# Start of a decoder layer: scale before shift, and the adaLN product's k tiles on four column strips

## The chip, the cores and the metric

The kernel runs on one core of one Trainium2 chip. The metric is device time in microseconds (us), the median of several runs. Five engines work side by side, each through its own instructions in order: TensorE (PE, with PEld for its weight loads), VectorE (DVE), ScalarE (ACT), GpSimd (POOL) and SyncE (SP), which here issues loads and stores.

## The reference

One decoder layer for 512 prompt rows and 8 sequences of 4 sample rows, 544 rows in all, of 1024 features each. Only its first steps are touched:

```python
def decoder_layer(x, c, pos, conv_buf, S0, attend, p):
    mod = jax.nn.silu(c) @ p['w_ada'] + p['b_ada']
    sh1, sc1, g1, sh2, sc2, g2, sh3, sc3, g3 = [m[:, None, :] for m in jnp.split(mod, 3 * N_SUB, axis=-1)]
    h = rmsnorm(x, p['ffn1_norm_pre']) * (1 + sc1) + sh1
    x = x + 0.5 * g1 * rmsnorm(swiglu(h, p['ffn1_w_gate'], p['ffn1_w_up'], p['ffn1_w_down']), p['ffn1_norm_post'])
...
```

The vector c has 9 rows (one for the prompt, eight for the samples), and w_ada is 1024 x 9216: nine segments of 1024 columns, of which segment 0 is sh1 and segment 1 is sc1. Everything is float32.

## The kernel before

x is held transposed, features on partitions: `xT` is 128 partitions x 8 blocks x 544 columns (a column is a row of x). Columns come in two halves of 272; the last 32 of the second half are the sample rows, whose modulation differs per sequence. A float32 matmul is done as three matmuls in a one-pass format (L301, `mm3`): weights and activations are each split into a high part and a rest (`hi`, `lo` of the weights, L270 on ACT and L271 on DVE; `hh`, `hl` of the activations).

The start of the layer, up to the steady feed-forward, is what the change touches. Its steps:

- Loads. SP issues c, the five pieces of x, then tiles `wb` of w_ada (128 x 512, 256 KB), then the first feed-forward weight tiles `raw`. ACT's queue issues nine small loads of gains, biases and convolution weights (`vraw`, `wraw`). Loads take one of eight completion semaphores each; a load that takes a semaphore again waits until the load that had it last has landed.
- x is turned by PE (`xps`, L507), copied to `xT`, and its squares are summed (`sqx`, L525). The sum over features is a matmul (`pre_s`, L366); DVE works out the reciprocal root in a chain of small operations (L340 to L345); PE spreads it over partitions (`pre_p`, L353 and L355, one tile for each column half).
- adaLN. `ada` multiplies the transposed silu(c) (`cT`, 32 columns of stationary weights per k tile) by w_ada. It is called with two pieces, (segment 1, half h) and (segment 0, half h): for each k tile one matmul for each piece, on two of TensorE's four 32-column strips (`adaps`, L467). After 8 k tiles the result goes through ACT (`ms`, L471) and is turned by PE (`adapt`, L474); DVE adds the bias and forms the scale (`modT`, L480 and L488). A float32 matmul shows as two records in the profile.
- Modulate (L536 to L551). For each block of 128 features and each column half: DVE multiplies x by scale and root (`mt`, L536), ACT adds the shift and rounds (`hh`, L538), DVE forms the rest (`hl`, L539). The 32 sample columns of each block take four small DVE steps and one on ACT (`ts`, L545 to L551).
- The feed-forward starts with block 0 of 11: four units of 24 matmuls each (`pg` and `pu` over features 0 to 511, then over 512 to 1023). It is issued behind the modulation but mixed into it by the compiler's order, and a coroutine `rest` adds the other seven segments of w_ada (`wa` tiles, four pieces a time) between the feed-forward's matmuls.

A half h of the feature blocks (0 to 3, then 4 to 7) goes through adaLN and modulate in turn.

Of the kernel before, what the change touches and what calls it, by code (L numbers as in the profile page):

```python
# [19 lines left out]
P = 128  # L20
# [7 lines left out]
ST = 4  # L28
# [208 lines left out]
class Layer:  # L237
# [170 lines left out]
    def load_vectors(self, sp):  # L408
        nc, a = self.nc, self.a
        v = sp.tile([112, P], F32, name="vraw")  # L410
        nc.scalar.dma_start(out=v[0:72, :], in_=a["b_ada"][0].rearrange("(b c) -> b c", c=P))
        gains = ("ffn1_norm_pre", "ffn1_norm_post", "mix_norm_pre", "mix_norm_post", "ffn2_norm_pre")
        for i, n in enumerate(gains):
            nc.scalar.dma_start(out=v[72 + 8 * i:80 + 8 * i, :], in_=a[n][0].rearrange("(b c) -> b c", c=P))
        w = sp.tile([105, P], F32, name="wraw")
        nc.scalar.dma_start(out=w[0:96, :], in_=a["conv_w"][0].rearrange("i (b c) -> (i b) c", c=P))
        nc.scalar.dma_start(out=w[96:97, :], in_=a["dn_norm"])
        nc.scalar.dma_start(out=w[97:105, :], in_=a["ffn2_norm_post"][0].rearrange("(b c) -> b c", c=P))
        return v, w

    def use_vectors(self, v, w):
# [26 lines left out]
    def ada(self, pieces, wa_pool, whole=True):  # L448
# [28 lines left out]
        for j, (seg, h) in enumerate(pieces):  # L477
            bs = slice(4 * h, 4 * h + 4)
            m = self.modT[:, seg, bs, :]
            nc.vector.tensor_tensor(  # L480
                out=m, in0=ptv[:, :, 32 * j:32 * j + 9],
                in1=self.vecs[:, seg * 8 + 4 * h:seg * 8 + 4 * h + 4].unsqueeze(2).to_broadcast([P, 4, 9]), op=ALU.add)
            kind, sub = seg % 3, seg // 3
            if kind:
                gv = self.gains[("ffn1_norm_", "mix_norm_", "ffn2_norm_")[sub] + ("pre" if kind == 1 else "post")]
                gb = gv[:, bs].unsqueeze(2).to_broadcast([P, 4, 9])
                if kind == 1:
                    nc.vector.scalar_tensor_tensor(out=m, in0=m, scalar=1.0, in1=gb, op0=ALU.add, op1=ALU.mult)  # L488
                else:
                    nc.vector.scalar_tensor_tensor(out=m, in0=m, scalar=1.0 if sub == 1 else 0.5, in1=gb,  # L490
                                                   op0=ALU.mult, op1=ALU.mult)

    def smod(self, seg, b0, b1):

# [1304 lines left out]
def layer(ctx, tc, a, dbg=None, stop=None):  # L1799
# [25 lines left out]
    mx.plan(feed)  # L1825
    with ExitStack() as c2:
        sp = L.pool("sp", 1, c2)
        vw = L.load_vectors(sp)
        L.load_cond(sp)
        L.load_x(sp)  # L1830
        wa = L.pool("wa2", 24, c2)
        ada0 = L.ada([(1, 0), (0, 0)], wa, False)
        for b in range(8):
            for c in range(2):
                L.sumsq(L.xT[:, b, :], sqx, b, tmp, c, nc.vector if b % 2 else None)
            if b % 2:
                next(ada0)
        rms0 = L.rms(sqx, (0, 1), "pre0")
        for i in range(4):
            next(ada0)  # L1840
            if i == 1:
                with tc.issue_after(L.ada_mm.ins):
                    next(rms0)
                    L.use_vectors(*vw)
        with tc.issue_after(L.ada_mm.ins):
            rps = drain(rms0)
        drain(ada0)
        for i in range(4):
# [134 lines left out]
```

## Time and profile before

| | us |
|---|---|
| median of 3 runs | 1587.06 |
| lowest and highest | 1586.16, 1587.81 |
| the profiled execution | 1590.33 |
| its span, first to last instruction | 1588.5 |

The profile is of one execution. Its span is the time from the first to the last instruction that it shows; 1.8 us of that run lie outside it. TensorE is busy for 95% of the span and its granted clock is 0.981 on the mean, so a microsecond saved where TensorE waits, early in the program, shortens the whole run by a microsecond if nothing later takes it back. The change touches only the first 60 us of code; from about 140 us on the instructions of each engine stand in the same order as before.

### The profile page before, as it was taken

Reading aid. Unit: us, or ns where it says so; the run is one execution under the profiler, and the core shown is the slowest. Engines: PE = TensorE matmul, PEld = TensorE weight load, DVE = VectorE, ACT = ScalarE, POOL = GpSimd, SP = SyncE. Lnnn points to the kernel's source line nnn. Section 1 sums busy time; section 2 is a strip of 40 time slices with the busy share of each in tenths; the row PEclk is TensorE's granted clock in tenths of the full one; section 3 lists DMA queues with packets and bytes.
Section 4 is the critical chain, followed back from the end, with each engine's and each line's share of the span. In section 5 each row is a group of like instructions: output and inputs, shape, how many; then the busy total and the mean of one; then the engine's idle time right before and its main releaser. Section 6 shows DMA issues by size and latency. Waiting matters only on the chain. (4 is left out here: it accounts for less than half of the span.)

```text
span 1588.5 us, 32490 instructions
## 1 busy us (share of the span) xinstructions
PE 1513.1 (95%) x12819; PEld 1408.5 (89%) x12819; DVE 846.5 (53%) x2080; ACT 633.5 (40%) x1397; POOL 293.7 (18%) x386
## 2 busy tenths in 40 slices
PE   7999999999998999998999999998989999999996
PEld 3898999999987999898788898896979999999995
DVE  5433322333488787468879658748374332233354
ACT  4222222222445554254675432233465332233363
POOL 1000000000353232123012112312548000000042
PEclk9999999999999999799999999999999999999998
DMA  9455454554656434554212325624426323333253
GB/s 323 140 172 179 129 160 141 160 158 136 197 162 194 115 89 105 127 146 112 48 44 67 99 69 133 160 78 131 139 67 167 107 82 92 91 91 87 83 148 102
DMA packets 314533, 199.64 MB, mean 126 GB/s; under 512 B 36464, under 2 KB 297331, under 8 KB 314092
## 3 DMA queue, kind: packets, MB, share of 16 engines
q1 hardware_dynamic: 314086, 197.46, 43.7%
q8 instruction: 100, 1.64, 0.4%
q14 instruction: 53, 0.43, 0.1%
q10 hardware_dynamic: 294, 0.11, 0.0%
HBM read 182.08 MB, written 16.36 MB: 125 GB/s over the span
## 5 line engine op out<-in xcount | busy, mean ns | idle before, releaser
L270 ACT CAST hi<-raw 128x512 fp32r<-128x512 f32 (+2 forms) x502 | 287.0, 581 | 592.7 <-PE pu L301 161.8
L271 DVE TENSOR_TENSOR lo<-raw,hi 128x512 fp32r<-128x512 f32 (+2 forms) x368 | 249.9, 681 | 436.0 <-ACT hi L270 416.9
L301 PE MATMUL pb<-hh,hi 128*128 128x272 f32 (+1 forms) x1008 | 234.6, 303 | 2.2 <-ACT hh L270 1.8
L301 PE MATMUL pb<-hh,lo 128*128 128x272 f32 (+1 forms) x1008 | 226.5, 295 | 2.3 <-DVE lo L271 2.3
L301 PE MATMUL pb<-hl,hi 128*128 128x272 f32 (+1 forms) x1008 | 225.3, 294 | 0.0
L271 POOL TENSOR_TENSOR lo<-raw,hi 128x512 fp32r<-128x512 f32 (+1 forms) x104 | 139.1, 1341 | 450.9 <-ACT hi L270 423.6
L301 PEld LDWEIGHTS pb<-hh,hi 128*128 128x128 f32 (+1 forms) x1008 | 165.4, 192 | 12.1 <-issue 4.5
L301 PE MATMUL pd<-fh,hi 128*128 128x272 f32 x704 | 171.8, 291 | 0.0
L301 PE MATMUL pd<-fl,hi 128*128 128x272 f32 x704 | 170.9, 290 | 0.0
L301 PEld LDWEIGHTS pb<-hh,lo 128*128 128x128 f32 (+1 forms) x1008 | 165.0, 192 | 5.3 <-DVE lo L271 2.5
L301 PEld LDWEIGHTS pb<-hl,hi 128*128 128x128 f32 (+1 forms) x1008 | 165.2, 191 | 2.6 <-issue 1.0
L301 PE MATMUL pd<-fh,lo 128*128 128x272 f32 x672 | 162.2, 289 | 0.8 <-POOL lo L271 0.8
L301 PE MATMUL pg<-hh,hi 128*128 128x272 f32 x672 | 149.7, 293 | 7.1 <-ACT hh L550 3.4
L301 PE MATMUL pu<-hh,hi 128*128 128x272 f32 x672 | 148.8, 292 | 1.6 <-ACT hi L270 1.6
L301 PE MATMUL pg<-hl,hi 128*128 128x272 f32 x672 | 147.8, 290 | 0.8 <-DVE hl L539 0.7
L301 PE MATMUL pu<-hl,hi 128*128 128x272 f32 x672 | 146.5, 289 | 0.0
L301 PE MATMUL pu<-hh,lo 128*128 128x272 f32 x672 | 146.0, 289 | 0.0
L301 PE MATMUL pg<-hh,lo 128*128 128x272 f32 x672 | 145.8, 289 | 0.0
L301 PEld LDWEIGHTS pd<-fh,hi 128*128 128x128 f32 x704 | 120.6, 189 | 8.4 <-issue 5.9
L301 PEld LDWEIGHTS pg<-hh,hi 128*128 128x128 f32 x672 | 108.8, 189 | 19.4 <-ACT hh L550 5.4
L301 PEld LDWEIGHTS pd<-fl,hi 128*128 128x128 f32 x704 | 120.9, 189 | 0.0
L301 PEld LDWEIGHTS pu<-hh,hi 128*128 128x128 f32 x672 | 108.7, 190 | 11.2 <-issue 5.9
(445 smaller groups left out, 2508.5 us busy)
## 6 DMA issues: line engine op xcount, KB each, us to landing
raw<-w_in SPq DMA_DIRECT2D x136, 256.0 KB
wa<-w_ada SPq DMA_DIRECT2D x56, 512.0 KB
raw<-ffn_w_gate SPq DMA_DIRECT2D x94, 256.0 KB
raw<-ffn_w_up SPq DMA_DIRECT2D x94, 256.0 KB
raw<-ffn_w_down SPq DMA_DIRECT2D x92, 256.0 KB
wb<-w_ada SPq DMA_DIRECT2D x32, 256.0 KB
S<-state_delta SPq DMA_DIRECT2D x8, 512.0 KB
delta_sample<-S SPq DMA_DIRECT2D x8, 512.0 KB
```

What stands on the lines that cost most here:

```text
L270: self.nc.scalar.copy(out=hi, in_=raw)
L271: (eng or self.nc.vector).tensor_tensor(out=lo, in0=raw, in1=hi.bitcast(F32), op=ALU.subtract)
L301: self.nc.tensor.matmul(out=ps[:m, c, :TH], lhsT=a[:r, kt, :m], rhs=b[:r, kx, c * TH:(c + 1) * TH], start=first and i == 0, stop=last and ...
```

## The change

Scale and shift are separate products now (`ada_piece`, one piece each), and x is multiplied by scale and root (`scaled`) before the shift is there. In a piece the 8 k tiles go to the four column strips in turn (strip k mod 4, two k tiles added up in each), and the four partial sums are added by the matmul that turns them: instead of a transposition by the identity it multiplies by `sel`, four 32 x 32 identities below each other. The sample columns of four blocks are handled at once, their shift and rest on GpSimd (`shifted`). The nine small loads go from ACT's queue to SP's, behind x and ahead of w_ada, and two `raw` tiles are fetched ahead of w_ada's second half instead of four.

```diff
@@ setup
+        self.sel = cp.tile([P, 32], F32, name="sel")
+        for j in range(0, P, 32):
+            nc.vector.tensor_copy(out=self.sel[j:j + 32, :], in_=self.ident[j:j + 32, j:j + 32])
...
@@ load_vectors
-        nc.scalar.dma_start(out=v[0:72, :], in_=a["b_ada"][0].rearrange("(b c) -> b c", c=P))
+        nc.sync.dma_start(out=v[0:72, :], in_=a["b_ada"][0].rearrange("(b c) -> b c", c=P))
...
+    def ada_piece(self, seg, h, wa_pool):
+        nc, a = self.nc, self.a
+        ps = self.wk("adaps")
+        for k in range(8):
+            wa = wa_pool.tile([P, 512], F32, tag="wb", name="wb")
+            nc.sync.dma_start(out=wa, in_=a["w_ada"][0, k * P:(k + 1) * P, seg * D + h * 512:seg * D + h * 512 + 512])
+            j = 32 * (k % 4)
+            self.ada_mm = nc.tensor.matmul(out=ps[j:j + 32, :], lhsT=self.cT[:, k, :], rhs=wa, start=k < 4, stop=k >= 4,
+                                           skip_group_check=True)
+            if k % 4 == 3:
+                yield
+        ms = wa_pool.tile([P, 512], F32, tag="ms", name="ms", bufs=2)
+        nc.scalar.copy(out=ms, in_=ps)
+        pt = self.wk("adapt")
+        for q in range(4):
+            nc.tensor.matmul(out=pt[:, 128 * q:128 * q + 32], lhsT=ms[:, q * P:(q + 1) * P], rhs=self.sel, start=True,
+                             stop=True)
+        self.ada_use(seg, h, pt.rearrange("p (q r) -> p q r", q=4)[:, :, 0:9])
...
+    def scaled(self, rps, h, sp):
...
+                nc.vector.scalar_tensor_tensor(out=t[:, :n], in0=self.xT[:, b, c * TH:c * TH + n],
+                                               scalar=self.modT[:, 1, b, 0:1], in1=rps[c][:, :n], op0=ALU.mult,
+                                               op1=ALU.mult)
+        bs = slice(4 * h, 4 * h + 4)
+        t = ts["s"] = sp.tile([P, 4, NS], F32, tag="tss", name="tss", bufs=2)
+        nc.vector.tensor_tensor(out=t, in0=self.xT[:, bs, SEQ:T],
+                                in1=rps[1][:, TH - NS:].unsqueeze(1).to_broadcast([P, 4, NS]), op=ALU.mult)
...
+    def shifted(self, ts, h, x):
...
+                nc.scalar.activation(out=hh[:, b, s], in_=ts[b, c][:, :n], func=AF.Identity, bias=sh)
+                nc.vector.scalar_tensor_tensor(out=hl[:, b, s], in0=ts[b, c][:, :n], scalar=sh,
+                                               in1=hh[:, b, s].bitcast(F32), op0=ALU.add, op1=ALU.subtract)
+            if b % 4 == 0:
+                t4 = ts["s"].rearrange("p b (s t) -> p b s t", t=ST)
+                nc.gpsimd.tensor_tensor(out=t4, in0=t4, in1=self.smod(0, bs.start, bs.stop), op=ALU.add)
+                nc.scalar.copy(out=hh[:, bs, SEQ:T], in_=ts["s"])
+                nc.gpsimd.tensor_tensor(out=hl[:, bs, SEQ:T], in0=ts["s"], in1=hh[:, bs, SEQ:T].bitcast(F32),
+                                        op=ALU.subtract)
...
@@ layer
-        vw = L.load_vectors(sp)
         L.load_cond(sp)
         L.load_x(sp)
+        vw = L.load_vectors(sp)
         wa = L.pool("wa2", 24, c2)
-        ada0 = L.ada([(1, 0), (0, 0)], wa, False)
+        pa, pb = L.ada_piece(1, 0, wa), L.ada_piece(0, 0, wa)
...
-        for i in range(4):
+        for i in range(2):
             feed.fetch(i)
-        for i in range(SPLIT_AHEAD):
-            feed.prep(i)
         for h in range(2):
             if h:
-                drain(L.ada([(1, h), (0, h)], wa, False))
-            for b in range(4 * h, 4 * h + 4):
-                for c in range(2):
-                    drain(L.modulate(rps[c], 0, tmp, x, c, b, b + 1))
+                drain(L.ada_piece(1, 1, wa))
+            ts = L.scaled(rps, h, sp)
+            if h:
+                drain(L.ada_piece(0, 1, wa))
+            else:
+                drain(pb)
+                for i in range(2):
+                    feed.prep(i)
+            L.shifted(ts, h, x)
```

SP's queue from x to the first tile of w_ada, before; the names DMAHW0 to DMAHW7 are the eight completion semaphores, and a wait on one is for the load that took it last:

```order
L503 DMA xn<-x_prompt 128x1024 [waits DMAHW1_49]
L503 DMA xn<-x_prompt 128x1024 [waits DMAHW4_49]
L503 DMA xn<-x_prompt 128x1024 [waits DMAHW5_49]
L503 DMA xn<-x_prompt 128x1024 [waits DMAHW6_49]
L503 DMA xn<-x_sample 32x1024 [waits DMAHW7_49]
L458 DMA wb<-w_ada 128x512 [waits DMAHW0_49]
```

The same place of the changed kernel:

```order
L584 DMA xn<-x_prompt 128x1024 x4
L584 DMA xn<-x_sample 32x1024
L414 DMA vraw<-b_ada 72x128
L417 DMA vraw<-ffn_norm_pre 8x128 [waits DMAHW0_49]
L417 DMA vraw<-ffn_norm_post 8x128 [waits DMAHW1_49]
L417 DMA vraw<-mix_norm_pre 8x128 [waits DMAHW2_49]
L417 DMA vraw<-mix_norm_post 8x128 [waits DMAHW3_49]
L417 DMA vraw<-ffn_norm_pre 8x128 [waits DMAHW4_49]
L419 DMA wraw<-conv_w 96x128 [waits DMAHW5_49]
L420 DMA wraw<-dn_norm 1x128 [waits DMAHW6_49]
L421 DMA wraw<-ffn_norm_post 8x128 [waits DMAHW7_49]
L503 DMA wb<-w_ada 128x512 [waits DMAHW0_49]
```

The waits on small loads are gone from x, and the small loads now wait for pieces of x, with w_ada behind them.

PE from the sum of squares to the first feed-forward matmul, before:

```order
L366 MATMUL pre_s<-ones,sqx 128x64 x6
L425 MATMUL vecps<-ident,vraw 128x112
L426 MATMUL vecps<-ident,wraw 128x105
L467 MATMUL adaps<-wb,cT 32x512 x4
L353 MATMUL pre_p<-ident,rms6y 128x128 x2
L355 MATMUL pre_p<-ident,rms6y 128x16
L353 MATMUL pre_p<-ident,rms6y 128x128 x2
L355 MATMUL pre_p<-ident,rms6y 128x16
L474 MATMUL adapt<-ident,ms 128x64 x4
L467 MATMUL adaps<-wb,cT 32x512 x2
L301 MATMUL pg<-hh,hi 128x272
L301 MATMUL pu<-hh,hi 128x272
```

The same place after the change:

```order
L428 MATMUL vecps<-ident,vraw 128x112
L429 MATMUL vecps<-ident,wraw 128x105
L513 MATMUL adapt<-sel,ms 128x32 x4
L505 MATMUL adaps<-wb,cT 32x512 x4
L353 MATMUL pre_p<-ident,rms6y 128x128 x2
L355 MATMUL pre_p<-ident,rms6y 128x16
L353 MATMUL pre_p<-ident,rms6y 128x128 x2
L355 MATMUL pre_p<-ident,rms6y 128x16
L513 MATMUL adapt<-sel,ms 128x32 x4
L505 MATMUL adaps<-wb,cT 32x512 x6
L301 MATMUL pg<-hh,hi 128x272
L301 MATMUL pu<-hh,hi 128x272
```

The scale is turned by itself, ahead of the last four tiles of the shift, and six tiles of the second half's scale stand ahead of the first feed-forward matmul.

DVE where modulate begins, before:

```order
L480 TENSOR_TENSOR modT<-adapt,vecs 128x36 x2
L271 TENSOR_TENSOR lo<-raw,hi 128x512
L488 SCALAR_TENSOR_TENSOR modT<-modT,vecs 128x36
L271 TENSOR_TENSOR lo<-raw,hi 128x512
L536 SCALAR_TENSOR_TENSOR mt<-xT,modT,pre_p 128x272
L271 TENSOR_TENSOR lo<-raw,hi 128x512 x2
L539 SCALAR_TENSOR_TENSOR hl<-mt,modT,hh 128x272
L536 SCALAR_TENSOR_TENSOR mt<-xT,modT,pre_p 128x240
L545 TENSOR_TENSOR ts<-xT,pre_p 128x32
L536 SCALAR_TENSOR_TENSOR mt<-xT,modT,pre_p 128x272
L539 SCALAR_TENSOR_TENSOR hl<-mt,modT,hh 128x240
L548 TENSOR_TENSOR ts<-ts,modT 128x32
```

After:

```order
L543 SCALAR_TENSOR_TENSOR mts<-xT,modT,pre_p 128x272
L543 SCALAR_TENSOR_TENSOR mts<-xT,modT,pre_p 128x240
L271 TENSOR_TENSOR lo<-raw,hi 128x512
L543 SCALAR_TENSOR_TENSOR mts<-xT,modT,pre_p 128x272
L271 TENSOR_TENSOR lo<-raw,hi 128x512
L543 SCALAR_TENSOR_TENSOR mts<-xT,modT,pre_p 128x240
L543 SCALAR_TENSOR_TENSOR mts<-xT,modT,pre_p 128x272
L543 SCALAR_TENSOR_TENSOR mts<-xT,modT,pre_p 128x240
L543 SCALAR_TENSOR_TENSOR mts<-xT,modT,pre_p 128x272
L543 SCALAR_TENSOR_TENSOR mts<-xT,modT,pre_p 128x240
L548 TENSOR_TENSOR tss<-xT,pre_p 128x128
L522 TENSOR_TENSOR modT<-adapt,vecs 128x36
```

All eight scale steps of the half now stand ahead of the shift's `modT` (L522), and the eight `hl` steps behind it.

## Rows read from the trace of the kernel before

**Rows 1.** The page's row of granted TensorE clock, tenths, 40 slices of 39.7 us.
```profile
PEclk9999999999999999799999999999999999999998
```

**Rows 2.** Windows: length, busy us (count) of PE, PEld, DVE, ACT, POOL; PEclk; DMA share; GB/s.
```profile
14.00:16.00 2.00, 2.00 (x11) 0.55 (x10) 0.94 (x3) 1.98 (x8) 0.58 (x1) 1.00 1.06 389
51.50:54.50 3.00, 3.00 (x15) 2.94 (x13) 2.96 (x12) 1.54 (x6) 0.00 (x0) 0.50 1.21 483
```

**Rows 3.** Timeline of the loads: start, length, engine, line, operation [idle before <-releaser].
```profile
0.73 0.34 SPq L438 DMA_DIRECT2D cn<-c_prompt  x1
2.12 4.04 SPq L503 DMA_DIRECT2D xn<-x_prompt  x4
...
6.67 11.61 SPq L458 DMA_DIRECT2D wb<-w_ada  x16
...
12.40 1.67 PE L507 MATMUL xps<-ident,xn 128*128 128x128 f32 x16 [0.63 <-DMA xn<-x_prompt]
...
20.70 0.14 PEld L467 LDWEIGHTS adaps<-wb,cT 128*32 128x32 f32 x2 [0.54 <-DMA wb<-w_ada]
...
21.68 1.55 PE L366 MATMUL pre_s<-ones,sqx 128*128 128x64 f32 x12
```

**Rows 4.** SP's waits in the first 60 us: total us, times, longest.
```profile
SPq L503 <- DMA vraw<-mix_norm_post: 1.3, 1, 1.3
...
SPq L503 <- DMA cn<-c_prompt: 0.7, 1, 0.7
```

**Rows 5.** Timeline, from the spread root to the first scale steps.
```profile
26.00 0.40 PE L353 MATMUL pre_p<-ident,rms6y 128*128 128x128 f32 x2 [0.73 <-ACT ms L471]
...
28.87 0.49 DVE L536 SCALAR_TENSOR_TENSOR mt<-xT,modT,pre_p 128x272 f32<-128x272 f32 x1
29.28 1.28 DVE L271 TENSOR_TENSOR lo<-raw,hi 128x512 fp32r<-128x512 f32 x2
29.39 0.52 ACT L538 ACTIVATE hh<-mt,modT 128x272 fp32r<-128x272 f32 x1 [1.40 <-DVE mt L536]
```

**Rows 6.** Timeline of DVE in the middle of modulate's first half.
```profile
34.01 0.49 DVE L536 SCALAR_TENSOR_TENSOR mt<-xT,modT,pre_p 128x272 f32<-128x272 f32 x1
34.42 0.18 DVE L549 TENSOR_TENSOR ts<-ts,modT 128x32 f32<-128x32 f32 x1
34.52 0.46 DVE L536 SCALAR_TENSOR_TENSOR mt<-xT,modT,pre_p 128x240 f32<-128x240 f32 x1
34.90 0.18 DVE L545 TENSOR_TENSOR ts<-xT,pre_p 128x32 f32<-128x32 f32 x1
```

**Rows 7.** Timeline of PE: adaLN matmuls between feed-forward matmuls, and the turn.
```profile
38.48 1.05 PE L467 MATMUL adaps<-wb,cT 128*32 128x512 f32 x4
...
40.41 1.05 PE L467 MATMUL adaps<-wb,cT 128*32 128x512 f32 x4
...
44.15 0.46 PE L474 MATMUL adapt<-ident,ms 64*128 64x64 f32 x4
...
54.69 1.07 PE L467 MATMUL adaps<-wa,cT 128*32 128x512 f32 x2
...
58.65 1.07 PE L467 MATMUL adaps<-wa,cT 128*32 128x512 f32 x8
```

**Rows 8.** Timeline of modulate's second half and the end of feed-forward block 0.
```profile
43.39 0.58 ACT L471 COPY ms<-adaps 64x512 f32<-64x512 f32 x1 [4.66 <-PE adaps L467]
...
49.94 0.39 PE L301 MATMUL pg<-hh,hi 128*128 128x272 f32 x1 [2.19 <-ACT hh L550]
...
55.22 0.19 DVE L551 TENSOR_TENSOR hl<-ts,hh 128x32 fp32r<-128x32 f32 x1 [0.28 <-ACT hh L550]
...
58.05 0.41 PE L301 MATMUL pu<-hl,hi 128*128 128x272 f32 x2
...
58.30 0.41 PE L301 MATMUL pu<-hh,lo 128*128 128x272 f32 x2
```

**Rows 9.** Timeline inside feed-forward block 5.
```profile
122.45 0.62 ACT L607 ACTIVATE sil<-pg 128x544 f32<-128x544 f32 x1 [8.78 <-PE pg L301]
...
123.64 0.52 PE L301 MATMUL pu<-hh,hi 128*128 128x272 f32 x2 [1.28 <-ACT hi L270]
```

**Rows 10.** A group of GpSimd over the span: busy us, mean ns of one.
```profile
L271 POOL TENSOR_TENSOR lo<-raw,hi 128x512 fp32r<-128x512 f32 (+1 forms) x104 | 139.1, 1341 | 450.9 <-ACT hi L270 423.6 <-ACT W L1474 19.2 <-PE psu L1340 4.4
```

More of the change, by code (lines that the diff above doesn't have):

```diff
@@ new lines, in ada_use @@
+    def ada_use(self, seg, h, src):
+        nc = self.nc
+        bs = slice(4 * h, 4 * h + 4)
+        m = self.modT[:, seg, bs, :]
+        nc.vector.tensor_tensor(
+            out=m, in0=src,
+            in1=self.vecs[:, seg * 8 + 4 * h:seg * 8 + 4 * h + 4].unsqueeze(2).to_broadcast([P, 4, 9]), op=ALU.add)
+        kind, sub = seg % 3, seg // 3
+        if kind:
+            gv = self.gains[("ffn1_norm_", "mix_norm_", "ffn2_norm_")[sub] + ("pre" if kind == 1 else "post")]
+            gb = gv[:, bs].unsqueeze(2).to_broadcast([P, 4, 9])
+            if kind == 1:
+                nc.vector.scalar_tensor_tensor(out=m, in0=m, scalar=1.0, in1=gb, op0=ALU.add, op1=ALU.mult)
+            else:
+                nc.vector.scalar_tensor_tensor(out=m, in0=m, scalar=1.0 if sub == 1 else 0.5, in1=gb,
+                                               op0=ALU.mult, op1=ALU.mult)
@@ new lines, in scaled @@
+    def scaled(self, rps, h, sp):
+        nc = self.nc
+        ts = {}
+        for b in range(4 * h, 4 * h + 4):
+            for c in range(2):
+                n = TH - c * NS
+                t = ts[b, c] = sp.tile([P, TH], F32, tag="mts", name="mts", bufs=8)
+                nc.vector.scalar_tensor_tensor(out=t[:, :n], in0=self.xT[:, b, c * TH:c * TH + n],
+                                               scalar=self.modT[:, 1, b, 0:1], in1=rps[c][:, :n], op0=ALU.mult,
+                                               op1=ALU.mult)
+        bs = slice(4 * h, 4 * h + 4)
+        t = ts["s"] = sp.tile([P, 4, NS], F32, tag="tss", name="tss", bufs=2)
+        nc.vector.tensor_tensor(out=t, in0=self.xT[:, bs, SEQ:T],
+                                in1=rps[1][:, TH - NS:].unsqueeze(1).to_broadcast([P, 4, NS]), op=ALU.mult)
+        t4 = t.rearrange("p b (s t) -> p b s t", t=ST)
+        nc.vector.tensor_tensor(out=t4, in0=t4, in1=self.smod(1, bs.start, bs.stop), op=ALU.mult)
+        return ts
@@ new lines, in shifted @@
+    def shifted(self, ts, h, x):
+        nc = self.nc
+        hh, hl = x
+        bs = slice(4 * h, 4 * h + 4)
+        for b in range(4 * h, 4 * h + 4):
+            for c in range(2):
+                n = TH - c * NS
+                s = slice(c * TH, c * TH + n)
+                sh = self.modT[:, 0, b, 0:1]
+                nc.scalar.activation(out=hh[:, b, s], in_=ts[b, c][:, :n], func=AF.Identity, bias=sh)
[7 more added lines that the diff above has]
+                                        op=ALU.subtract)
@@ L1835, in layer @@
                 L.sumsq(L.xT[:, b, :], sqx, b, tmp, c, nc.vector if b % 2 else None)
-            if b % 2:
-                next(ada0)
+            if b % 4 == 3:
+                next(pa)
         rms0 = L.rms(sqx, (0, 1), "pre0")
-        for i in range(4):
[L1840 to L1844, printed above, removed]
+        next(pb)
+        with tc.issue_after(L.ada_mm.ins):
+            next(rms0)
+            L.use_vectors(*vw)
+            drain(pa)
+        next(pb)
         with tc.issue_after(L.ada_mm.ins):
             rps = drain(rms0)
-        drain(ada0)
-        for i in range(4):
+        for i in range(2):
             feed.fetch(i)
-        for i in range(SPLIT_AHEAD):
-            feed.prep(i)
         for h in range(2):
             if h:
-                drain(L.ada([(1, h), (0, h)], wa, False))
-            for b in range(4 * h, 4 * h + 4):
-                for c in range(2):
-                    drain(L.modulate(rps[c], 0, tmp, x, c, b, b + 1))
+                drain(L.ada_piece(1, 1, wa))
+            ts = L.scaled(rps, h, sp)
+            if h:
+                drain(L.ada_piece(0, 1, wa))
+            else:
+                drain(pb)
+                for i in range(2):
+                    feed.prep(i)
+            L.shifted(ts, h, x)
     fp = env["fp"] = L.pool("fp", 1, c1)
```

8 lines of the change are left out of this document (4 added, 4 removed).

## The prediction

> **What bounds the kernel now.** The page comes first: TensorE works in nearly every slice, so the question is what it waits for at the start, and whether later stages take a gain back. The windows come next. In the steady load stage the transfers run at 389 GB/s [rows 2]. Then the timeline, in which three stretches are to be seen.
>
> *Up to 21.68 us* the loads decide. PE takes the w_ada tiles in order and waits for each: the twelfth comes at 20.70, and the sum of squares, which stands behind it in PE's order, starts at 21.68 [rows 3]. A tile of 256 KB at 389 GB/s takes 0.67 us, so, counted back eleven tiles, the first landed at about 13.3. I call 21.68 S and give times as S plus.
>
> *From S to the end of feed-forward block 0* (58.65, S+36.97 [rows 7]) first the root and the modulation decide, then PE, which has the second half's adaLN mixed into the feed-forward, then DVE, which is done with the second half only at 55.41 [rows 8]. PE then has its last matmuls to do.
>
> *After that* PE is nearly always busy. One wait there depends on the order on ACT: inside block 5 PE waits 1.28 us for a cast that stands behind an activation [rows 9].
>
> **The change, part by part.**
>
> *Loads (shift of S).* Now SP's loads of x wait for small loads of ACT's queue: 1.3 us for one of them, and 0.7 us for c [rows 4]; the fourth piece lands at about 12.4 [rows 3]. Changed, x follows c at once, from about 1.5 us. A lone load of 4 KB took 1.39 us from issue to landing (0.73 to 2.12, where the load that waited for it starts [rows 3, 4]). The 2.2 MB of x take 5.7 us at 389 GB/s, so x lands at 1.5+1.4+5.7 = 8.6 at the earliest, at 12.4 if nothing is won; I take 9.4, nearer the early end, since nothing else is in flight then. The nine small loads then stand between: the last but one waits for the last piece of x, and behind it on SP are one more small load, all w_ada tiles and all feed-forward tiles. Two issues at 0.35 are 0.7. The first tile then needs 1.39+0.67 = 2.1 at least and about 3.5 if the fixed part doubles; I take 2.8. So it lands at 12.9 (bounds 11.4 and 16.6) against 13.3. The tiles behind it come at the same pace. I take 0 for S: the 0.4 is within what I can't read, and the bounds are -1.9 and +3.3. What x wins is lost again, because SP's queue runs dry before w_ada. The squares don't decide: x being earlier, they are done before the twelfth tile.
>
> [...]
>
> *Root and scale.* New in DVE's chain of small operations is the scale's bias, which waits for the turn of the scale by PE. That turn is no transposition any more: four matmuls of two records each, 0.13 a record (12 in 1.55 [rows 3]), 0.92 instead of 0.46 [rows 7]. It stands behind the two turns of the vectors and ends at about S+2.8, so the chain's later half comes 0.4 late; behind it on DVE are the rest of the root and all scale steps. The spread root, now at 26.00 (S+4.3 [rows 5]), comes at S+4.75, the first scale step at S+5.3, where it is S+7.2 now. Starts 0.41 and 0.38 apart [rows 6], eight scale steps are 3.2; two `lo` in between 1.3 [rows 5]; the sample step 0.2 and the shift's bias 0.1. So the first `hh` starts at S+10.1 (now 29.39, S+7.7 [rows 5]) and PE's first feed-forward matmul at S+10.7. That is later than now, because the order puts all eight scale steps ahead of the shift.
>
> *PE's stretch.* From there PE has 48 matmuls at 0.125 (two starts 0.25 apart [rows 8]), 6.0. A round of adaLN costs the same for one, two or four strips: two matmuls (four records) take 1.05, four take 1.07, one takes 1.07 [rows 7]. In the pattern of now, 38.48 to 40.41 with six feed-forward matmuls between, a round costs 1.93-0.75 = 1.18. The strips would make two rounds of eight tiles, but the order gives more: in this stretch tiles 6 and 7 of the scale stand alone, then come a round of four, one of two, and two alone: 6 x 1.18 = 7.1 (now 8 rounds, two already before the first feed-forward matmul). The turn of the second scale is 0.9, and 0.3 is the wait for ACT's copy of the last sum (0.58 [rows 8], half hidden). Together S+10.7+14.3 = S+25.0, then the turn of the shift and its bias: S+26.1.
>
> *Second half of modulate.* Its scale steps are done by then, hidden under PE's stretch. DVE has four `lo` (2.5) and eight `hl` (3.2) and waits about 0.3 for ACT: S+32.0, where it is S+33.7 now. The sample columns have left DVE: some 2 us a half. Then 22 matmuls and a hand-over, 2.9: block 0 ends at S+35.0, not S+36.97. That is -2.0. Before, a round of `rest` is inside (54.69 [rows 7]); after, none is, but the order holds six groups of its first 16 tiles instead of seven, so nothing is owed later.
>
> *GpSimd.* Two operations of 128 columns a half; the third `hh` of ACT waits for one, and behind it are six more. From 1341 ns for 512 columns [rows 10] it is 0.34 by columns and 1.34 if size doesn't matter; at 0.45 ACT finds it done, at 1.34 block 0 ends 1.6 later. I take 0.
>
> *ACT's order in block 5.* The wait of now goes (-1.28). In its place the copy of block 5's product stands ahead of the first cast of block 6: product on DVE, copy and cast on ACT, three operations like the 0.62 one [rows 9], with hand-overs 1.9. That is +0.6.
>
> *Clock.* [...] After, PE is idle from about S+8 to S+10.7. [...] I take 0.8.
>
> Sum: 0 - 2.0 + 0 + 0.6 + 0.8 = -0.6 us. The profiled execution's 1590.33 becomes 1589.7; on the scale of the median, 1587.06, 3.3 below that execution, 1586.4.
>
> **The rivals.**
>
> *Faster: separate adaLN matmuls overlap with the feed-forward.* If PE ran a lone strip beside other matmuls, five of the six rounds would cost about 0.5 instead of 1.18: -3.4, in all -4.0, 1583.1. Against it: the lone one at 54.69 took 1.07. An early w_ada (-1.9) without a slow clock (-0.8) would come to -3.3 too, 1583.8.
>
> *No gain, loads late.* x is not earlier than now: the first tile at 12.4+0.7+2.8 = 15.9, +2.6, in all +2.0, 1589.1. For it: nine small loads ahead of w_ada; against it: x no longer waits for any.
>
> [...]
>
> **How the numbers follow.** 0.2% is 3.2 us, about what a measurement of this kernel can tell from no change. The sum, with its unknowns, has 0.51: 1586.4, its own range 1584.0 to 1589.0. Loads late 0.12 (1589.1, within 0.2%). Overlap, or loads early with the clock up, 0.24 (faster, 1583). Clock 0.13 (slower, 1590.7). So faster 0.24, same 0.63, slower 0.13. The range leaves out a tenth on each side: 1582.4 to 1590.6.
>
> **What would show it.** The profile after should have the sum of squares within 1 us of 21.7, DVE's first scale step at about S+5.3 with eight in a row, the first feed-forward matmul near S+10.7 (later than now), the shift's second bias at S+26, block 0 done at S+35, and a wait of about 1.9 between blocks 5 and 6. The prediction is wrong if w_ada's first tile lands outside 11.4 to 16.6, if a GpSimd step takes over 1.4, or if rounds of one strip cost less than 1 us.

## The result and the profile after

The changed kernel takes 1596.41 us (median of 7 runs, 1592.22 to 1601.73) against 1587.06 (7 runs, 1583.0 to 1589.83): ratio 1.0064, interval 1.0041 to 1.0087. In 12 more runs it took 1597.03 against 1587.99, with a ratio of 1.0055 (1.0032 to 1.0077). It is slower by about 9 us, where 0.7 us less was forecast. The profiled execution took 1599.76, its span is 1598.0, and its mean granted clock 0.978 (before: 1588.5 and 0.981).

From the page of the kernel after: the granted clock in 40 slices of 40 us (it answers to [rows 1]), and the queue that the page calls instruction, taken here as PE's code (loads, MB, share of 16 engines).

```profile
PEclk9999999999999999799899999998999999999999
q8 instruction: 101, 1.65, 0.4%
```

The 17th, 20th and 28th slice stand below 9; before it was the 17th and the last. The loss is not in one place. The start comes first: SP's waits in its first 62 us, kernel after (total us, times, longest; [rows 4] answers to it).

```profile
SPq L503 <- DMA wb<-w_ada: 7.3, 19, 1.2
SPq L417 <- DMA xn<-x_prompt: 3.6, 2, 2.7
SPq L419 <- DMA xn<-x_prompt: 1.3, 1, 1.3
```

Windows of the kernel after: length, busy us (count) of PE, PEld, DVE, ACT, POOL; PEclk; DMA share; GB/s.

```profile
10.00:13.00 3.00, 2.52 (x25) 2.24 (x23) 2.04 (x4) 2.51 (x7) 0.00 (x0) 1.00 0.18 43
14.00:16.00 2.00, 1.56 (x4) 0.28 (x4) 1.28 (x3) 1.71 (x6) 1.55 (x3) 1.00 0.93 293
16.00:20.00 4.00, 3.01 (x8) 0.55 (x8) 2.69 (x5) 2.11 (x6) 3.02 (x4) 1.00 1.01 341
20.00:24.00 4.00, 4.00 (x13) 0.83 (x12) 0.11 (x1) 0.59 (x1) 0.00 (x0) 1.00 1.05 398
```

Between x and w_ada the transfers fall to 43 GB/s for three microseconds: small loads wait for pieces of x, and w_ada waits behind the small loads. Then w_ada begins at 293 GB/s and reaches before's 389 [rows 2] only at 20 us.

Timeline of the kernel after (start, length, engine, line, operation [idle before <-releaser]); it answers to [rows 3], [rows 5] and [rows 7 to 9].

```profile
1.48 1.78 SPq L584 DMA_DIRECT2D xn<-x_prompt  x4
10.65 0.32 SPq L419 DMA_DIRECT2D wraw<-conv_w  x1
11.65 9.58 SPq L503 DMA_DIRECT2D wb<-w_ada  x16
14.44 1.63 PE L505 MATMUL adaps<-wb,cT 128*32 128x512 f32 x4 [1.91 <-DMA wb<-w_ada]
16.53 0.14 PEld L505 LDWEIGHTS adaps<-wb,cT 128*32 128x32 f32 x2 [1.37 <-DMA wb<-w_ada]
18.91 0.14 PEld L505 LDWEIGHTS adaps<-wb,cT 128*32 128x32 f32 x2 [1.44 <-DMA wb<-w_ada]
23.63 0.14 PEld L505 LDWEIGHTS adaps<-wb,cT 128*32 128x32 f32 x2 [0.52 <-DMA wb<-w_ada]
24.61 1.55 PE L366 MATMUL pre_s<-ones,sqx 128*128 128x64 f32 x12
29.65 0.87 DVE L543 SCALAR_TENSOR_TENSOR mts<-xT,modT,pre_p 128x272 f32<-128x272 f32 x2 [0.72 <-PE pre_p L355]
34.41 0.91 ACT L564 ACTIVATE hh<-mts,modT 128x272 fp32r<-128x272 f32 x2 [4.46 <-DVE modT L522]
34.68 0.41 POOL L569 TENSOR_TENSOR tss<-tss,modT 128x128 f32<-128x128 f32 x1 [15.22 <-DVE tss L551]
34.99 0.39 PE L301 MATMUL pg<-hh,hi 128*128 128x272 f32 x1 [1.37 <-ACT hh L564]
50.51 0.20 DVE L522 TENSOR_TENSOR modT<-adapt,vecs 128x36 f32<-128x36 f32 x1 [4.39 <-PE adapt L513]
53.46 0.40 PE L301 MATMUL pg<-hh,hi 128*128 128x272 f32 x1 [1.24 <-ACT hh L570]
54.00 2.66 DVE L565 SCALAR_TENSOR_TENSOR hl<-mts,modT,hh 128x272 fp32r<-128x272 f32 x6
54.45 0.59 PE L301 MATMUL pg<-hl,hi 128*128 128x272 f32 x1 [0.47 <-POOL hl L571]
61.36 0.41 PE L301 MATMUL pu<-hh,lo 128*128 128x272 f32 x2
114.19 0.42 PE L301 MATMUL pu<-hh,lo 128*128 128x272 f32 x2
129.89 0.52 PE L301 MATMUL pg<-hh,hi 128*128 128x272 f32 x2 [2.08 <-ACT hi L270]
1031.60 0.18 PE L1540 MATMUL pt<-W,X 32*32 32x32 f32 x1 [1.06 <-issue]
```

The sum of squares starts at 24.61, so S is 2.93 later here. The next steps behind it stand within 0.4 us of where the working had them: the first scale step at S+5.04, the first `hh` at S+9.80, the first feed-forward matmul at S+10.4, the second shift's bias at S+25.9, DVE's last `hl` of the second half done at S+32.05. The end of block 0 does not: its last matmul, the second of the row at 61.36, starts at 61.48, S+36.87, where before it was at S+36.75 and S+35.0 was forecast for the block's end. The wait between blocks 5 and 6 is 2.08 us on PE. The last row has no place in the prediction: PE waits 1.06 us in the middle of the delta rule (a later step of the layer), about 900 us behind the last instruction that the change reorders, and the profile names no engine and no load that released it.

Two more numbers from many executions. The mean granted clock is listed for each run, and 122 runs of the kernel before, taken on three chips beside those of the experiments, lie along one line (with a scatter of 1.6 us): 1591.6 us at a clock of 0.980 (uncertain by 0.15), 1.31 us less for each 0.001 more; their mean clock is 0.9824. So a kernel's loss splits into what is left **at equal clock** (each run moved along that line to 0.980, then the mean) and what the lower clock costs. The 19 runs of the changed kernel have 1594.5 at equal clock, 2.9 over before, and a mean clock of 0.9781, 0.0043 lower, which the line makes 5.6 us. Together 8.5.

| kernel | runs | median us | ratio (interval) | mean clock | at clock 0.980 |
|---|---|---|---|---|---|
| before | 122 | 1587.9 | | 0.9824 | 1591.6 |
| after, again | 12 | 1597.03 | 1.0055 (1.0032, 1.0077) | 0.9781 | 1594.4 |
| e1_vec_act | 12 | 1594.55 | 1.003 (1.0008, 1.0052) | 0.9777 | 1591.3 |
| e4_vec_pool | 12 | 1596.39 | 1.0034 (1.001, 1.0058) | 0.9762 | 1590.8 |
| e8_feed4 | 12 | 1594.47 | 1.0034 (1.0015, 1.0053) | 0.9784 | 1592.8 |
| e2_before_vec_sp | 12 | 1591.17 | 1.0011 (0.9988, 1.0034) | 0.9816 | 1593.8 |
| e3_before_hold | 12 | 1590.56 | 1.0012 (0.9985, 1.0038) | 0.9812 | 1593.3 |
| e5_strips | 6 | 1602.02 | 1.0089 (1.0059, 1.0118) | 0.9757 | 1597.4 |
| e6_scaled | 12 | 1591.03 | 1.0022 (0.9996, 1.0048) | 0.9798 | 1591.5 |
| before_pad12 | 12 | 1592.28 | 1.0035 (1.0018, 1.0051) | 0.9786 | 1591.0 |
| before_pad64 | 12 | 1591.95 | 1.0023 (1.0001, 1.0044) | 0.9801 | 1592.2 |
| after_pad52 | 12 | 1593.83 | 1.0042 (1.0021, 1.0064) | 0.9794 | 1593.4 |
| before_split48 | 12 | 1591.06 | 1.0011 (0.9979, 1.0042) | 0.9796 | 1591.2 |
| before_split256 | 12 | 1587.39 | 0.9993 (0.9963, 1.0023) | 0.9828 | 1591.8 |
| after_split208 | 12 | 1593.58 | 1.0034 (1.0006, 1.0062) | 0.9796 | 1592.7 |

The mean clock of 12 runs is uncertain by about 0.001, the time at equal clock by about 0.5 us.

### The profile page after: what moved, and what is told of

Read it like the earlier page. It is cut to its first block, busy times and chain, and to the rows that moved or that the text cites. A ratio compares the mean times of both kernels' runs of the same rounds, so it can differ in the third digit from the quotient of the medians.

```text
span 1598.0 us, 32520 instructions
## 1 busy us (share of the span) xinstructions
PE 1519.6 (95%) x12843; PEld 1414.6 (89%) x12843; DVE 844.6 (53%) x2056; ACT 634.6 (40%) x1393; POOL 298.6 (19%) x390
## 3 DMA queue, kind: packets, MB, share of 16 engines
q8 instruction: 101, 1.65, 0.4%
## 5 line engine op out<-in xcount | busy, mean ns | idle before, releaser
L301 PEld LDWEIGHTS pu<-hh,hi 128*128 128x128 f32 x672 | 108.3, 189 | 10.4 <-issue 6.7
```

The source lines that it names most:

```text
L301: self.nc.tensor.matmul(out=ps[:m, c, :TH], lhsT=a[:r, kt, :m], rhs=b[:r, kx, c * TH:(c + 1) * TH], start=first and i == 0, stop=last and ...
```

## The experiments

### Where the loads stand

The changed kernel, the vectors (the nine small loads) back on ACT's queue ahead of c and x (e1):

```diff
-        nc.sync.dma_start(out=v[0:72, :], in_=a["b_ada"][0].rearrange("(b c) -> b c", c=P))
+        nc.scalar.dma_start(out=v[0:72, :], in_=a["b_ada"][0].rearrange("(b c) -> b c", c=P))
...
+        vw = L.load_vectors(sp)
         L.load_cond(sp)
         L.load_x(sp)
-        vw = L.load_vectors(sp)
```

> The changed kernel with the nine small loads back on ACT's queue, ahead of c and x. Theory (the loads cost the early part of the loss): the sum of squares starts at 21.7 us as before, not 24.6, and block 0 ends 2.9 us earlier than in the changed kernel, at about 57.6; the time is about 1593.5 if the rest of the loss stays where it is, 1587 if the later stretches of low clock only follow the late start. Rival (the strips and the scale-before-shift order cost it): the sum of squares moves but the end of block 0 stays near 60.5 and the time near 1596.

Timeline, changed kernel with the vectors on ACT's queue:

```profile
14.12 7.97 PE L505 MATMUL adaps<-wb,cT 128*32 128x512 f32 x24
22.02 1.22 PE L366 MATMUL pre_s<-ones,sqx 128*128 128x64 f32 x9
```

The twelve tiles go through PE without a gap, the sum of squares is back at 22.02, and block 0's last matmul starts at 58.87, 2.6 earlier than in the changed kernel (61.48). At equal clock the kernel stands at 1591.3, 3.1 under the changed one. The loads' place costs that much; the mean clock stays low (0.9777).

The kernel before with only the vectors moved, by the same edit the other way round (e2):

> The kernel before with only the nine small loads moved to SP's queue behind x. Theory: the sum of squares starts at about 24.6 us, block 0 ends at 61.6, and the time is 1590.0 if 2.9 us is all that it costs, 1593 to 1596 if the low clock later in the program comes with it. Rival (the loads cost nothing because x is there earlier): sum of squares at 21.7, time 1587.

Its start, in the same windows as above, and the sum of squares:

```profile
10.00:13.00 3.00, 2.76 (x25) 2.48 (x23) 1.84 (x4) 2.27 (x6) 0.00 (x0) 1.00 0.28 77
14.00:16.00 2.00, 1.62 (x4) 0.25 (x4) 1.28 (x3) 1.71 (x6) 1.49 (x2) 1.00 0.93 292
...
23.96 1.22 PE L366 MATMUL pre_s<-ones,sqx 128*128 128x64 f32 x9
```

The gap and the slow first tiles are there without the rest of the change. S is 2.1 later than the mean of three profiles of before (21.68, 22.16, 21.82), the time at equal clock 2.2 higher, and the clock (0.9816) that of before. So the loads cost their own length and no clock.

The kernel before, held back by four loads that nobody reads (e3):

```diff
+        for k in range(4):
+            pad = wa.tile([P, 512], F32, tag="pad", name="pad", bufs=4)
+            nc.sync.dma_start(out=pad, in_=a["w_ada"][0, k * P:(k + 1) * P, 0:512])
```

> The kernel before with four more loads of 256 KB, which nobody reads, ahead of w_ada on SP's queue: at 0.68 us each they hold the start back by 2.7 us and change nothing else. If a late start by itself brings more low clock later in the program, the time is 1593 to 1596; if a late start costs its own length, 1589.8.

The sum of squares starts at 23.89, 2.0 later, and the time at equal clock is 1.7 higher, with a clock of 0.9812. A late start costs its own length; it does not bring the lower clock (0.9816 and 0.9812 in these two kernels, each uncertain by about 0.001, against 0.9820 in the 35 runs of before beside them).

The changed kernel with the vectors on GpSimd's queue (`nc.gpsimd.dma_start` in `load_vectors`, e4):

> The changed kernel with the nine small loads on GpSimd's queue. Theory (the gap between x and w_ada, 16 to 60 GB/s from 10 to 13 us, is the cost): SP's queue has w_ada right behind x, the first tile lands at 10.5 to 11.5 instead of 14.4, the sum of squares starts at 20 to 21 (the squares, done at 20.1 in the changed kernel, then decide), and the time is 4 us under the changed kernel's, 1592, or 1588 if the later clock losses go with it. Rival (many small loads slow the queue wherever they stand): the sum of squares at 23 or later, time 1594 to 1597.

Window and timeline of that kernel:

```profile
10.00:13.00 3.00, 3.00 (x22) 2.83 (x20) 1.37 (x3) 1.67 (x4) 0.00 (x0) 1.00 1.05 336
...
3.76 13.40 SPq L503 DMA_DIRECT2D wb<-w_ada  x16
...
20.65 1.42 PEld L366 LDWEIGHTS pre_s<-ones,sqx 128*128 128x128 f32 x12 [0.94 <-DVE sqx L606]
```

w_ada is issued from 3.76 us right behind x, there is no gap, and the squares decide at 20.65. At equal clock this is the best version of the change, 1590.8, 0.8 under before (uncertain by 0.5). Its clock is 0.9762, and its median is as late as the changed kernel's. The gap is the cost; the small loads on a queue of their own are not.

### Which part of the change lowers the clock

Strips alone: adaLN in single pieces on four strips, all of both pieces ahead of modulate, the old modulate and the old loads (e5):

```diff
...
-                drain(L.ada([(1, h), (0, h)], wa, False))
+                drain(L.ada_piece(1, h, wa))
+                drain(L.ada_piece(0, h, wa))
...
```

> The kernel before with the adaLN products of the start as single pieces on four strips, summed by the turn; modulate, the nine small loads and the four raw tiles stay as they were. ACT's order in block 5 is that of the changed kernel. If the strips and the order that comes with them lower the granted clock, its mean over the runs is 0.978 as in the runs with the changed body (before: 0.982), the wait between blocks 5 and 6 is 2.4 us, and the median is 1593 to 1595. If the other part (scale before shift, sample columns on GpSimd) lowers it, the mean is 0.982 and the median 1589 to 1591.

Mean clock 0.9757, and 5.8 over before at equal clock: block 0's last matmul starts at S+42.6 (64.34 against 21.73), six later than before's S+36.75. Pieces without the new modulate are a loss of their own. The wait between blocks 5 and 6 is there (2.1 us).

Modulate alone: `scaled` and `shifted` with adaLN in pairs, the old loads (e6):

```diff
...
-            for b in range(4 * h, 4 * h + 4):
-                for c in range(2):
-                    drain(L.modulate(rps[c], 0, tmp, x, c, b, b + 1))
+            ts = L.scaled(rps, h, sp)
+            L.shifted(ts, h, x)
...
```

> The kernel before with modulate in the new form alone (all scale steps of a half first, sample columns of four blocks at once with GpSimd for shift and rest); adaLN stays in pairs, the loads as they were. Its order is that of before from block 1 on, with the 1.28 us wait inside block 5. If this part lowers the clock: mean 0.978, median 1592 to 1594. If the strips do: mean 0.982 and block 0 ends 1 to 2 us earlier than before (DVE has less to do), median 1586.5 to 1588.

PE's wait inside block 5 stays before's 1.3 us (`pu` for `hi`), the clock is 0.9798, between the two, and block 0 does not end earlier (61.51, with 10.2 us at a granted clock of 0.50, the lower of the two levels in the trace, ahead of 140 us). At equal clock nothing is gained or lost (1591.5).

The two raw tiles: the kernel of e1 with four fetched and two split where before had them (e8):

```diff
-        for i in range(2):
+        for i in range(4):
             feed.fetch(i)
+        for i in range(SPLIT_AHEAD):
+            feed.prep(i)
...
             else:
                 drain(pb)
-                for i in range(2):
-                    feed.prep(i)
```

> The changed kernel with the small loads back on ACT's queue and with four raw tiles fetched, and two split, ahead of the second half, as before. If the two raw tiles instead of four cause the order on ACT that makes PE wait 2.4 us between blocks 5 and 6, that wait is gone and the median falls by about 2 us under the one with the loads alone (1594.55). If it comes from the adaLN order, the wait stays at 2.4 and the median within 1 us of 1594.5; the mean clock stays at 0.978 in both cases.

The wait between blocks 5 and 6 stays at 2.1 us, so ACT's order there comes from adaLN's order, not from the raw tiles; clock 0.9784, median as e1's; at equal clock it is 1.5 over e1 (uncertain by 0.8).

The changed kernel again:

> The changed kernel itself once more, for more runs of it beside those of the others: median 1596 to 1597, mean clock 0.978. At equal clock (0.980) it should stand 3.5 to 4 us over the kernel before (1591.7 by a line through its 35 runs) if the late start and the longer wait behind block 5 are all that it costs there; the remaining 5 us would be the lower clock.

1597.03, clock 0.9781, 1594.4 at equal clock, 2.8 over before where 3.5 to 4 was expected.

### More profiles of the two kernels

> The kernel before once more, for a second profile of it. If the stretches of low clock behind 140 us belong to a kernel, they stand where they stood (one of 3.4 us at 775, 17 us at 655, none at 940 to 1030) and add up to 58 us from 140 us on; if they fall by chance from one execution to the next, places and lengths change, anywhere from 45 to 75.

> The changed kernel once more, for a third profile. If the stretches of low clock belong to the kernel, it has 10 us of them at 778 and some at 918 and 945 to 970 again, 68 us from 140 us on; if they fall by chance, as with the kernel before, 45 to 75, and its lower mean clock (0.978 against 0.982) has to come from more such chances ahead of 140 us.

> The kernel before, a third profile, with the same two expectations as for the second: 58 us of low clock behind 140 us at the same places, or 45 to 75 at changing ones.

> The changed kernel, a fourth profile, with the same two expectations as for the third: 68 us of low clock behind 140 us at the same places, or 45 to 75 at changing ones.

Four single executions: 1585.7 and 1590.39 for before, 1599.63 and 1600.93 for after. Time at the lower clock (0.50) behind 140 us, added up from the granted clock in the trace: before 57.8, 50.0 and 56.8; after 67.6, 69.4, 76.2 and 68.4. Places and lengths change from one execution to the next: at 655 to 672 us before had 17 us of it in the first profile and none at that place in the second. Yet the two groups don't overlap. Three windows of before (first fence) and of after (second), columns as above; from 140 us on the instructions of every engine stand in the same order in both, some 9 us later in the second, so the counts in a window differ a little:

```profile
760.00:900.00 140.00, 131.88 (x1444) 112.69 (x1444) 118.31 (x429) 90.24 (x274) 23.64 (x48) 0.99 0.24 60
900.00:1060.00 160.00, 156.06 (x1742) 145.64 (x1742) 105.08 (x299) 50.05 (x126) 37.51 (x42) 0.99 0.43 113
1060.00:1200.00 140.00, 123.55 (x1011) 115.84 (x1010) 91.90 (x212) 66.75 (x144) 63.08 (x59) 0.95 0.37 108
```

```profile
760.00:900.00 140.00, 131.32 (x1249) 111.27 (x1249) 115.23 (x431) 88.52 (x268) 24.68 (x48) 0.96 0.24 59
900.00:1060.00 160.00, 154.54 (x1893) 142.99 (x1884) 107.68 (x307) 49.23 (x123) 36.58 (x40) 0.98 0.43 112
1060.00:1200.00 140.00, 123.42 (x1008) 115.48 (x1008) 85.85 (x200) 61.18 (x133) 55.53 (x54) 0.94 0.36 104
```

What does differ there is PE's wait at `pt`; its other waits vary by up to about 1 us from one execution to the next. The wait at `pt` stands in all four profiles of the changed kernel and in e1, e4, e5 and e8, 0.7 to 1.9 us long, and in none of the profiles of before, e2, e3 and e6. These have as many PE instructions as before. The changed kernel has 12843 matmul records and as many weight loads on its page, before 12819: 48 instructions more. The code queue moved 1.65 MB in 101 loads (before 1.64 in 100): 16 KB a load. Taken as PE's code and divided by its 25.7 thousand instructions, that is an estimated 64 bytes each, 256 in a block of 16 KB. By that estimate 48 more move the borders of all blocks behind them.

The times of that queue's loads bind the wait to it. Each load is one packet of 16384 bytes. In all ten profiles with the wait (these eight and the two below with 48 more), such a load ends 1.27 to 1.54 us before PE goes on, in the profile above at 1030.24 for 1031.60, and the load before it ended 16 to 18 us earlier.

The wait is not where most of the lower clock stands, however. From 140 to 1015 us, ahead of it, the four profiles of the changed kernel have 41.0, 41.0, 41.0 and 34.1 us at the lower level and the three of before 30.7, 23.9 and 27.3; from 1015 on 26.6, 28.4, 35.3 and 34.2 against 27.1, 26.1 and 29.4. So 12 of the 15.6 us more, on the mean, stand ahead of the wait, as the first of the three windows shows. Right behind the wait, 0.2 to 2.2 us after PE goes on, a stretch of 3.4 or 6.8 us at the lower level begins in four of the ten profiles with it, and in none of the ten without.

### Borders of the code blocks

Twelve matmuls of 32 x 4 at the very start, 48 PE instructions that nobody needs, in the kernel before; 52 of them (208, with the change's 48 a whole block) in the changed kernel; 64 (a whole block, the control) in the kernel before. No other instruction changes its place:

```diff
+        ps = self.wk("padps")
+        for _ in range(12):
+            nc.tensor.matmul(out=ps[0:32, 0:4], lhsT=self.ones[:, 0:32], rhs=self.ones[:, 0:4], start=True, stop=True)
```

> The kernel before with 12 small matmuls (32 x 4, nobody reads them) at the very start of PE's program, while PE waits for c: 48 more PE instructions, as many as the change adds, and nothing else. Theory (PE's code comes in blocks of 16 KB, and 48 instructions more move the borders of all blocks behind them, so that PE waits for a block at a place where it did not): PE waits about 1 us with no releaser shown at the product pt near 1020 us, the mean clock over the runs falls from 0.982 to about 0.978, and the median is 1593 to 1596. Rival (the lower clock comes from the early stage of the changed kernel): no such wait, mean clock 0.982, median 1587 to 1590.

> The changed kernel with 52 such small matmuls at the start, 208 PE instructions: with its own 48 that is 256, which at 64 bytes each is one whole block, so all borders behind stand as in the kernel before. Theory: the wait of 1 us at pt near 1031 us is gone, the mean clock rises from 0.978 to 0.982, and the median is 1590 to 1592.5, what the late start and the wait behind block 5 cost and no more. Rival: wait or no wait, the clock stays at 0.978 and the median at 1595 to 1598.

> The kernel before with 64 small matmuls at the start, 256 PE instructions, one whole block: the control for the small matmuls themselves. Theory: the borders stand as in the kernel before, no wait at pt, mean clock 0.982, median 1587 to 1590. If the small matmuls themselves disturb the clock or the start, it is 1592 or more, like the one with 12.

The wait follows the borders as estimated: with 12 it is there, as the first row below from the kernel before with them shows; with 52 in the changed kernel and with 64 in the kernel before it is gone. The next two rows are from the kernel before itself, at the same place, without a wait.

```profile
1020.69 0.21 PE L1462 MATMUL pt<-W,X 32*32 32x32 f32 x1 [0.75 <-issue]
...
1022.04 0.25 PE L1456 MATMUL pz<-X,W 32*32 32x32 f32 x8
1022.10 0.24 PE L1459 MATMUL pt<-W,X 32*32 32x32 f32 x6
```

The time is not as clear. With 12 the clock falls to 0.9786, but the control has 0.9801 and is itself 4 us slower, 0.6 of it at equal clock (its sum of squares starts at 22.65); why its clock is lower, no run shows. The changed kernel with 52 has 0.9794, where 0.982 or 0.978 was expected. Hence the next three, where PE's additional instructions come from matmuls that are cut, while PE waits for w_ada. Cut so, the sums over adaLN's k tiles don't come out as the reference's, so the three serve for timing alone; instructions and transfers are as told, and that other values leave the clock as it is was not tested.

```diff
-                self.ada_mm = nc.tensor.matmul(out=ps[32 * j:32 * j + 32, :], lhsT=self.cT[:, k, :], rhs=was[j],
-                                               start=k == 0, stop=k == 7, skip_group_check=True)
+                w = 256 if not whole and h == 0 and k < 6 else 512
+                for q in range(0, 512, w):
+                    e = min(512, q + w)
+                    self.ada_mm = nc.tensor.matmul(out=ps[32 * j:32 * j + 32, q:e], lhsT=self.cT[:, k, :],
+                                                   rhs=was[j][:, q:e], start=k == 0, stop=k == 7,
+                                                   skip_group_check=True)
```

(48 more; with 104 for 256 and all k, 256 more; the like for 13 tiles of the changed kernel, 208 more.)

> The kernel before with 12 of the start's adaLN matmuls cut into two halves of 256 columns each, where PE waits for w_ada anyway: 48 more PE instructions, as in the changed kernel, without PE work at the start that the small matmuls brought (their control lost 4 us as well). Theory (borders of PE's code blocks): a wait of about 1 us with no releaser at pt near 1020 us, mean clock 0.978 to 0.979, median 1592 to 1594. Rival (the borders make the wait, but the clock comes from elsewhere): the wait is there, the clock stays at 0.982 to 0.983 and the median at 1588.5 to 1590.

> The control: 16 of the start's adaLN matmuls of the kernel before cut into five pieces each, 256 more PE instructions, one whole block. Theory: no wait at pt, mean clock 0.982 to 0.983, median 1587 to 1590. If the number of instructions as such, wherever the borders stand, lowers the clock, it is 0.980 and the median 1591 or more, as with the 64 small matmuls.

> The changed kernel with 13 of its first adaLN matmuls cut into five pieces, 208 more PE instructions, 256 with its own 48. Theory: no wait at pt, mean clock 0.981 to 0.983, median 1590 to 1592.5. Rival: no wait at pt, clock at 0.978 to 0.979, median 1594 to 1597.

The kernel before with 48 more has the wait:

```profile
1016.80 0.18 PE L1463 MATMUL pt<-W,X 32*32 32x32 f32 x1 [0.70 <-issue]
```

The other two don't. The control is the kernel before in time and clock (1587.39, clock 0.9828, 1591.8 at equal clock). With 48 the clock is 0.9796, which is neither the theory's value nor the rival's, and the median (1591.06) is not told from before's. In the changed kernel the borders' old place gives 0.9796 instead of 0.9781, where the theory had at least 0.981. There are four such comparisons, small matmuls or cut ones, in either kernel: 0.0015, 0.0032, 0.0013 and 0.0015 of clock, all of one sign, each only one or two of its uncertainties (about 0.0012 to 0.0016), and the last two share the runs of the changed kernel. That is 0.0019 on the mean (uncertain by about 0.0008), 2.5 us by the line. Single profiles don't follow it: behind 140 us the kernel before with 48 more, which has the wait, was 36.6 us at the lower level, and the changed kernel with 52 small matmuls and the kernel before with 64, which have none, 76.2 and 73.8.

## Why the prediction was wrong

**"I take 0 for S" failed**, the first large step. Its terms: x was taken to land at 9.4; the wait for its last prompt piece ended at 10.65, where `conv_w` is issued, and two small loads came behind it (10.51, 9.37 and 9.34 in the other three profiles). Issue of w_ada: 10.1 forecast, 11.65 measured. From issue to the first matmul 2.8 was taken and 2.79 measured (11.65 to 14.44). "The tiles behind it come at the same pace" was the larger miss: from 14.40 to 23.63 the twelve tiles' weight loads are 0.84 apart instead of 0.67: w_ada starts on an empty queue (43 GB/s ahead of it), and its transfers run at 293 and 341 GB/s in the windows (389 before). S came 2.93 later in that profile, 1.9 on the mean of four profiles (24.61, 24.22, 22.75, 23.61) against three of before. e1, e2 and e4 show that the place of the small loads does it, and that it is worth 2 to 3 us. "What x wins is lost again" was the right mechanism with too small a size; the rival of late loads had put 2.6 on S, the nearest of all.

**The body's sum came out nearly right, its largest term did not.** From S to the first matmul of block 6 before needs 106.48 us (128.16 less 21.68), after 105.28 (129.89 less 24.61), with one adaLN round of 1.05 [rows 7] still owed ("nothing is owed later" was wrong): about nothing won, where -2.0, +0.6 and +0.8 came to -0.6. "Then 22 matmuls and a hand-over, 2.9" failed. DVE was done at S+32.05, as forecast, but 34 matmuls of block 0 were left then, partly at a granted clock of 0.50, so the block ended no earlier than before. PE had waited 1.24 us at 53.46 for the sample columns and 0.47 behind it, and 3.4 us at 0.50 from 54.5 on fell upon its own work. No run shows the sum's clock term of 0.8 as such; these 3.4 us stand in its place, and half of them, 1.7, is what they cost by an estimate. Of the 2.0 that block 0 was to give, 0.5 is seen at the end of block 4, where the last `pu` (the second of its row) starts at S+90.19 before and at S+89.70 after, with as many adaLN matmuls done in both, in five rounds before and in four after. The wait behind block 5 is 2.08 in all four profiles against 1.28: +0.8 where +0.6 was said. GpSimd's steps took 0.41 to 0.92 us, below the 1.34 at which they were to cost something; the second half paid for them all the same, because the sample columns' `hh` stands behind other work of ACT there (1.24 us). At equal clock e1, which is the body without the loads, is 0.3 under before (uncertain by 0.7). The rows of the kernel before for the end of block 4 and the first matmul of block 6 (the kernel after has them at 114.19 and 129.89):

```profile
111.74 0.42 PE L301 MATMUL pu<-hh,lo 128*128 128x272 f32 x2
128.16 0.41 PE L301 MATMUL pg<-hh,hi 128*128 128x272 f32 x2
```

**Nothing stood in the prediction for what lies behind 140 us**, and most of the loss is there. The sum ends with the wait behind block 5 and puts the rest at nothing, because the order of instructions from there on is the same. That step failed: the order is the same, and still the mean clock is 0.0043 lower, 5.6 us by the line. A late start is not the reason (e2, e3: 0.9816, 0.9812). The clock's chance, 0.13 at 1590.7, has no run behind it; measured were 1596.41 and, ahead of 140 us, 3.4 us at the lower level in three of four profiles of the changed kernel and 10.2 in the fourth. What is shown: with 48 more PE instructions PE waits 0.7 to 1.9 us in a run of short matmuls, and with 256 more, or with as many as before, it doesn't; that a code block's border stands there is the author's estimate, from 256 instructions a block. What the four comparisons point to but don't show: some 2.5 us of the 5.6 hang on the borders. The wait at `pt` itself can't make most of the lower clock, since 12 of the 15.6 us more at the lower level stand ahead of it, and it is PE's only wait behind 140 us to which the profile gives no releaser. What stays open: why the clock is lower, and the other 3 us altogether. e6 (0.9798, borders as before) and after_split208 (0.9796, borders put back) have a lower clock than before, too. Both have 10.2 us at the lower level ahead of 140 us in their profile, before has 3.4 to 6.8; 3.4 to 6.8 us more at 0.50 lower a run's mean clock by an estimated 0.001 to 0.002 (half of them in some 1590 us), but one profile each does not settle it.

**The chances**: same 0.63 and slower 0.13 gave too little room to two losses at once; the bounds of S (-1.9 to +3.3) held the value, yet the range was made as if the far end would not come together with a loss of clock.

No version beat the kernel before. The one that came nearest at equal clock (vectors on GpSimd's queue, 1590.8) was not tried with the borders put back.

## What to carry to other kernels

Keep a queue from running dry between two large loads: here small loads that waited for completions of the first were better on another queue (1591.3 us at equal clock on ACT's and 1590.8 on GpSimd's instead of 1594.4), and the price was not only the gap (43 GB/s from 10 to 13 us) but the slower pace of the first tiles behind it (0.84 us a tile instead of 0.67). When a kernel's runs differ by 1%, list time against the granted clock first: with a line through many runs, a 2 us cost can be read in a spread of 20. And an edit early in a long straight program can bring a wait far behind it, as 48 more PE instructions did here, with 0.7 to 1.9 us some 900 us later; where PE runs through many short matmuls, count its instructions before and after, and look for waits to which the profile gives no releaser.

## What the runs showed of the hardware

In ten profiles PE waited 0.7 to 1.9 us in a run of short matmuls, where by the estimate a border between two 16 KB blocks of its code stands: in the run of `pz` and `pt` the next eight records start 0.13 us after the last eight. At that pace, with as many weight loads, 256 instructions last an estimated 1.0 to 1.2 us (28 to 32 in 0.13 us), no longer than the 1.19 us that the load at 1029.05 took, where in the feed-forward, at one matmul in 0.125 us [rows 8], they last an estimated 16 us. In those ten profiles PE went on 1.27 to 1.54 us after the load of 16384 bytes had ended. The rows of the changed kernel:

```profile
1029.73 0.24 PE L1537 MATMUL pz<-X,W 32*32 32x32 f32 x8
1029.80 0.24 PE L1540 MATMUL pt<-W,X 32*32 32x32 f32 x6
1029.86 0.24 PE L1537 MATMUL pz<-X,W 32*32 32x32 f32 x8
1030.30 0.23 PE L1540 MATMUL pt<-W,X 32*32 32x32 f32 x4
```

The same program took 1580 to 1600 us over 122 runs on three chips (1580.6 to 1599.8 in 29 runs on one of them), and the mean granted clock went with it, from 0.974 to 0.988, along the line with its scatter of 1.6 us: most of that spread is clock.
